# Sixteen of 256 tokens taken out of the dense first expert product in both layers, their gathered dots issued in steps on separate tiles

## Chip, core and metric

One core of a Trainium2 chip runs the whole program. The metric is device time in microseconds (us) of one execution. Three runs of the kernel before took 1743.48, 1745.44 and 1746.33 us, so the median is 1745.44 us. One further execution was taken by the profiler: it took 1742.17 us, and its span from the first to the last instruction is 1740.5 us.

## What is computed

A trunk of two layers for 256 tokens of width 1024. Each layer mixes tokens and then sends each token through a retrieval over 16384 single-neuron experts, cut here to what matters:

```python
def block(t):                                   # PEER, per 128 tokens
    q = (t @ w_pq).reshape(T, 8, 2, 128)
    s = einsum('thpk,hpnk->thpn', q, sub_keys)
    ...                                         # top 16 of 128 keys, twice; top 16 of their pairs
    gate = softmax(best_s)
    u = expert_down[experts]                    # (T, 8, 16, D): 128 chosen experts a token
    act = gelu(einsum('td,thkd->thk', t, u))
    vv = expert_up[experts]
    return einsum('thk,thkd->td', gate * act, vv)
```

## The kernel before

The kernel doesn't gather `expert_down` for most tokens. It multiplies all 16384 rows of it with all tokens, applies the gelu, and multiplies the result with a gate that is zero for experts that weren't chosen.

**The first product** (`experts`, the loop over `i` from 0 to 127, here called tiles). A tile is 128 experts. Its 128x1024 matrix comes by DMA (SP's queue), ACT casts it to a high part `hi` (L245), DVE subtracts to get a low part `lo` (L238), and PE makes 24 products of 128x128 weights with `width` token columns (L317 hi, L318 lo, L319 hi again, for eight slices of D). Casts are kept about two tiles ahead of PE, in three buffers. Two tiles are a pair and share a PSUM bank. After each pair ACT takes the gelu of the bank: L1030 and L1033 for tokens 0 to 191, L1022 for those from 192 on, which L1023 stores to DRAM as `act_rows`. `FT` gives `width` by layer.

**The fill.** While the first tiles run, DVE still works off the retrieval of the experts (top keys, candidates, ranks; `run_fill`), which ends in `to_picks` with the chosen experts and gates. Only then do gates start. In layer 0, DVE also makes 48 conditioning dots (L203) among the tiles from 24 on; in layer 1 only 8.

**Gates.** For tokens 0 to 191, in 48 groups of four, GpSimd (POOL) makes four one-hots of 128x128 (L992), DVE makes three more tiles (L995, L997 twice), PE multiplies them (L1005, L1006, eight products a group) and DVE and ACT use the result (L1013, L1016, L1041). There are two buffers for one-hots, so group g+2's are made after group g's products.

**The remaining 64 tokens** are not gated densely. Their 128 chosen rows of `expert_up` are fetched by POOL with indirect DMAs (`fetch`, L1074), 128 of them in a layer, and their activations are read back out of `act_rows` (`fetch_act`, L1081).

**The dot path.** With `width` 240, the last 16 tokens are left out of the dense product. In layer 1 before, their 16x128 activations come by gathering: 128 partitions hold 16 tokens by 8 heads, and each of 16 steps `k` gathers 128 rows of `down_rows`, 512 KB, with an indirect DMA on POOL (`dot_fetch`, L949) into one of three buffers `R_DOTS`, and multiplies and sums it with the tokens' own rows `R_DX` on DVE (`dot`, L955). Gather k+3 goes to the buffer of dot k, so it waits for it. To get `R_DX`, DVE adds the two halves of the tokens (L933), PE transposes them in eight products (L937), ACT copies them (L938), and ACT's queue writes them to DRAM and reads them back eight times (L939, L943). The ranks take the same way (L940, L944), and DVE makes row numbers of them (L945, the wait of the first gather). Afterwards ACT takes the gelu (L959) and eight more DMAs bring the activations to where the second product uses them (L965). `dot_start` issues all of the preparation at one tile, `dot_step` a dot every two and a half tiles.

**What sets the order.** The program states the work in the order above, but a scheduler moves each instruction to the earliest place that its own model of time allows, by engine, except where `manual_schedule` holds. Each engine then works its queue strictly in that order. So the tile at which the program writes a step bounds it little; the built order tells where it stands.

## Time and profile before

| | |
|---|---|
| profiled execution, its span | 1742.17 us, 1740.5 us |
| median of three runs | 1745.44 us |
| busy: PE, DVE, ACT, POOL | 1702.8, 1454.1, 906.4, 878.6 us |
| first product of layer 0 (width 256), first to last pair's gelu | 196.8 to 583.9 us |
| first product of layer 1 (width 240), first to last pair's gelu | 1047.7 to 1434.4 us |
| one dot on DVE, one gather's issue on POOL, mean | 1257 ns, 1408 ns |
| a gather from issue to landing, median | 6.3 us |

A group's row in the lists reads: line, engine, operation, output<-input, shape, count | busy us, mean ns of one | the engine's idle time just before them and what ended it. A row of the timeline reads: start us, length us, engine, line, operation, count, and in brackets the idle time before it. In the table of windows each stretch has its length, then busy us and the number of instructions of each engine, then PE's granted clock (1.00 is full), the DMA share and GB/s. The two layers' first products are the same work but for width and the dot path, so their stretches can be laid side by side.

### The profile page before, as it was taken

What the parts mean: (1) busy time and instruction counts of PE and PEld (TensorE: products, weight loads), DVE (VectorE), ACT (ScalarE), POOL (GpSimd) and SP (SyncE); (2) the same over time, 40 slices, a digit from 0 to 9 for tenths busy, and PEclk for the clock granted to TensorE, in tenths of its full rate; (3) what the DMA queues carried; (4) which work ended last, traced back from release to release, by engine and by line L of the source; (5) the groups of instructions that cost most, each with busy time, mean ns of one, the idle gap of its engine ahead of it and who ended that gap; (6) DMA issues with size and microseconds to landing.
All of it is one profiled execution on the core that took longest, in us unless ns stands there. A gap on an engine that the chain in (4) does not pass through costs nothing.

```text
span 1740.5 us, 32411 instructions
## 1 busy us (share of the span) xinstructions
PE 1702.8 (98%) x11856; PEld 1556.9 (89%) x11856; DVE 1454.1 (84%) x2722; ACT 906.4 (52%) x1472; POOL 878.6 (50%) x713
## 2 busy tenths in 40 slices
PE   7999999999999999999999999998899999999998
PEld 6889999999999888888888999997899998888887
DVE  6858998788889799999966699957878877999996
ACT  2446455555444555555557555553455455555553
POOL 1000206588998477676100012339989847877630
PEclk9999999999999999999999999998999999999999
DMA  9965578888878799999843556677866667999993
GB/s 381 339 237 173 163 209 280 304 261 255 258 249 262 238 349 402 366 354 384 324 151 121 170 160 181 213 241 239 290 206 194 211 202 252 394 399 350 369 371 114
DMA packets 162563, 461.94 MB, mean 265 GB/s; under 512 B 51586, under 2 KB 53010, under 8 KB 161251
## 3 DMA queue, kind: packets, MB, share of 16 engines
q1 hardware_dynamic: 99936, 363.38, 61.6%
q0 software_dynamic: 26240, 88.36, 13.6%
q10 hardware_dynamic: 36226, 8.13, 2.2%
q8 instruction: 93, 1.52, 0.4%
q14 instruction: 68, 0.55, 0.1%
HBM read 449.16 MB, written 10.57 MB: 264 GB/s over the span
## 4 chain that ended last, share of the span: by engine, by line
PE 85%; DVE 9%; DMA 3%; issue 1%; ACT 1%; POOL 1%; ACTq 0%; SPq 0%; DVEq 0%; POOLq 0%
PE acc L1115 34%; PE ch L317 13%; PE ch L318 13%; PE ch L319 12%; DVE lo L238 3%; PE ch L315 3%; DMA arena<-in_down_rows,arena 1%; PE ch L398 1%; PE g L1005 1%; PE g L1006 1%; DMA raw<-in_w_ada 1%; PE acc L317 1%; PE acc L319 1%; PE acc L318 1%; DVE arena L780 1%
## 5 line engine op out<-in xcount | busy, mean ns | idle before, releaser
L245 ACT CAST hi<-raw 128x1024 fp32r<-128x1024 f32 x554 | 582.1, 1051 | 611.1 <-PE ch L319 318.4
L238 DVE TENSOR_TENSOR lo<-raw,hi 128x1024 fp32r<-128x1024 f32 x554 | 675.8, 1225 | 152.4 <-ACT hi L245 150.5
L318 PE MATMUL ch<-hh,lo 128*128 128x256 f32 (+1 forms) x2336 | 657.2, 281 | 11.9 <-DVE lo L238 11.8
L317 PE MATMUL ch<-hh,hi 128*128 128x256 f32 (+1 forms) x2336 | 661.7, 284 | 1.8 <-ACT ungated L1022 1.8
L319 PE MATMUL ch<-hh,hi 128*128 128x256 f32 (+1 forms) x2336 | 654.2, 280 | 0.0
L992 POOL TENSOR_SCALAR arena<-iota,picks 128x128 f16<-128x128 f16 x384 | 451.7, 1193 | 184.2 <-PE g L1006 82.1
L318 PEld LDWEIGHTS ch<-hh,lo 128*128 128x128 f32 x2336 | 443.7, 190 | 14.5 <-DVE lo L238 14.3
L317 PEld LDWEIGHTS ch<-hh,hi 128*128 128x128 f32 x2336 | 443.2, 190 | 2.3 <-ACT ungated L1022 2.0
L319 PEld LDWEIGHTS ch<-hh,hi 128*128 128x128 f32 x2336 | 443.7, 190 | 0.0
L1115 PE MATMUL acc<-hi,hh 128*128 128x512 f32 x1536 | 400.1, 395 | 0.0
L1115 PEld LDWEIGHTS acc<-hi,hh 128*128 128x128 f32 x1536 | 289.2, 188 | 67.3 <-DVE hh L1056 0.2
L1115 PE MATMUL acc<-lo,hh 128*128 128x512 f32 x1024 | 280.9, 395 | 0.0
L1074 POOL DMA_INDIRECT arena<-in_up,arena x128 | 184.3, 1440 | 107.3 <-DVE arena L1111 79.1
L1115 PEld LDWEIGHTS acc<-lo,hh 128*128 128x128 f32 x1024 | 192.9, 188 | 45.0
L1081 POOL DMA_INDIRECT arena<-act_rows,arena x128 | 178.8, 1397 | 83.2 <-PE acc L1115 45.1
L1111 DVE SCALAR_TENSOR_TENSOR arena<-arena 128x1024 f32<-128x1024 f32 x126 | 162.0, 1286 | 2.0 <-DMA arena<-in_up,arena 2.0
L203 DVE SCALAR_TENSOR_TENSOR raw<-raw,arena 128x1024 f32<-128x1024 f32 x96 | 116.8, 1221 | 9.9 <-DMA raw<-in_w_ada 5.8
L794 POOL CAST arena<-arena 128x512 f16<-128x512 uint32 x32 | 29.2, 926 | 139.2 <-DVE arena L783 107.6
L997 DVE TENSOR_TENSOR arena<-arena,parts 128x512 f16<-128x512 f16 x192 | 77.2, 441 | 21.4 <-PE g L1005 21.4
L758 POOL DMA_DIRECT2D arena<-in_keys x2 | 1.1, 562 | 169.7 <-issue 117.2
L1016 ACT ACTIVATE arena<-g 128x344 f32<-128x344 f32 (+23 forms) x96 | 31.1, 324 | 82.1 <-DVE arena L1013 80.3
L1056 DVE TENSOR_TENSOR hh<-arena,hh 128x768 fp32r<-128x768 f32 (+1 forms) x66 | 61.6, 933 | 0.9 <-ACT hh L1054 0.9
(243 smaller groups left out, 1656.5 us busy)
## 6 DMA issues: line engine op xcount, KB each, us to landing
raw<-in_down SPq DMA_DIRECT2D x256, 512.0 KB, 4.4
raw<-in_up SPq DMA_DIRECT2D x256, 512.0 KB, 6.3
raw<-in_w_ada SPq DMA_DIRECT2D x96, 512.0 KB, 4.9
raw<-in_w_pq SPq DMA_DIRECT2D x32, 512.0 KB, 3.8
raw<-in_w_in SPq DMA_DIRECT2D x26, 512.0 KB, 4.4
raw<-in_w_out SPq DMA_DIRECT2D x16, 512.0 KB, 3.9
act_rows<-ungated ACTq DMA_DIRECT2D x64, 64.0 KB, 4.7
arena<-in_w_in SPq DMA_DIRECT2D x6, 512.0 KB, 9.2
```

What stands on the lines that cost most here:

```text
L203: op = nc.vector.scalar_tensor_tensor(raw, raw, 1.0, cact, op0=OP.mult, op1=OP.mult, accum_out=mods[layer][:, col:col + 1])
L238: nc.vector.tensor_sub(lo, raw, hi.bitcast(F32))
L245: nc.scalar.copy(hi, raw)
L317: nc.tensor.matmul(dst, hi[:, cols], k[0], start=start, stop=False, **kw)
L318: nc.tensor.matmul(dst, lo[:, cols], k[0], start=False, stop=False, **kw)
L319: nc.tensor.matmul(dst, hi[:, cols], k[1], start=False, stop=stop, **kw)
L992: nc.gpsimd.tensor_scalar(oh[:, i, :], iota, picks[:, t:t + 1], None, op0=OP.is_equal)
L997: nc.vector.tensor_tensor(og[j], on, wide(1 + j), op=OP.mult)
L1074: nc.gpsimd.indirect_dma_start(out=R_ROWS[slots[k]], out_offset=None, in_=rows, in_offset=bass.IndirectOffsetOnAxis(ap=where_row[:, k:k + ...
L1081: nc.gpsimd.indirect_dma_start(out=R_ACTS[:, k % (2 * GROUP), :width - T], out_offset=None, in_=act_rows[layer][:, :], in_offset=bass.Indi ...
L1111: nc.vector.scalar_tensor_tensor(R_SUM, v, w8[:, k:k + 1], R_SUM, op0=OP.mult, op1=OP.add)
L1115: nc.tensor.matmul(acc[piece], w, u[:, lo:hi], start=piece not in opened, stop=last, skip_group_check=True)
```

## The change

`FT` becomes 240 in both layers, so layer 0 gets the dot path too. The bundle `dot_start` is cut into steps: `dot_rows` at tile 4, the store of the rows at tile 6, `dot_spread` at tile 9; after the fill (tile `start`) the store of the ranks, `dot_ranks` two tiles later, `dot_where` four later, the first three gathers at five, six and seven. Dot k stands at `start + 9 + 25k/8` and issues gather k+3 itself. Gelu and read-back follow. Three small regions move to another place in the arena, so that they can be written while the fill runs.

```diff
-FT = (S, 240)
+FT = (240, 240)
+DOT_STEP = 25
...
-        def dot_start():
+        def dot_rows():
             nc.vector.tensor_add(R_DH, hh[:, 0, :, width:].bitcast(F32), hh[:, 1, :, width:].bitcast(F32))
             for half in range(2):
...
                 nc.scalar.copy(R_DX[:alone, half * 512:(half + 1) * 512], ps[:alone, :])
-            nc.scalar.dma_start(dot_in, R_DX[:alone, :])
-            nc.scalar.dma_start(dot_ids, chosen[P - alone:, 0, :])
+        def dot_spread():
             for h in range(8):
-                t = slice(h * alone, (h + 1) * alone)
-                nc.scalar.dma_start(R_DX[t, :], dot_in)
-                nc.scalar.dma_start(R_DIX[t, 0, :], dot_ids[:, 16 * h:16 * h + 16])
+                nc.scalar.dma_start(R_DX[h * alone:(h + 1) * alone, :], dot_in)
+        def dot_ranks():
+            for h in range(8):
+                nc.scalar.dma_start(R_DIX[h * alone:(h + 1) * alone, 0, :], dot_ids[:, 16 * h:16 * h + 16])
+        def dot_where():
             nc.vector.tensor_scalar(R_DIX[:, 1, :].bitcast(U32), R_DIX[:, 0, :], float(layer * P * P), None,
                                     op0=OP.add)
+            nc.vector.memset(R_DA, 0.0)
...
                                            accum_out=R_DIX[:, 2, k:k + 1])
+            if k + 3 < 16:
+                dot_fetch(k + 3)
...
-            if n % 5 or n < 0:
-                return
-            k = n // 5
-            if k == 0:
-                dot_start()
-                for m in range(3):
-                    dot_fetch(m)
-            elif 3 <= k < 19:
-                dot(k - 3)
-                if k < 16:
-                    dot_fetch(k)
-            elif k == 19:
-                dot_end()
+        def dot_plan(start):
+            plan = {start: [lambda: nc.scalar.dma_start(dot_ids, chosen[P - alone:, 0, :])],
+                    start + 2: [dot_ranks], start + 4: [dot_where]}
+            for k in range(3):
+                plan[start + 5 + k] = [lambda k=k: dot_fetch(k)]
+            for k in range(16):
+                plan.setdefault(start + 9 + k * DOT_STEP // 8, []).append(lambda k=k: dot(k))
+            end = start + 9 + 15 * DOT_STEP // 8
+            plan[end + 1] = [dot_acts]
+            plan[end + 3] = [dot_back]
+            return plan
+        dots = {}
+        if alone:
+            dots = {4: [dot_rows], 6: [lambda: nc.scalar.dma_start(dot_in, R_DX[:alone, :])], 9: [dot_spread]}
...
-            if alone and start is not None:
-                for n in range(2):
-                    dot_step(2 * (i - start) + n)
+            if alone and start == i + 1:
+                dots.update(dot_plan(i + 1))
+            for fn in dots.pop(i, ()):
+                fn()
```

How the built order moves. POOL's queue in layer 0, kernel before, from the end of the fill: L992 is the one-hots, L1074 the fetches of `expert_up` rows, L1081 the reads of activations in the second product.

```order
L893 DMA x_dram<-arena 128x2048
L794 CAST arena<-arena 128x512 x16
L992 TENSOR_SCALAR arena<-iota,picks 128x128 x12
L1074 DMA arena<-in_up,arena 128x1024 x4
L992 TENSOR_SCALAR arena<-iota,picks 128x128 x180
L1081 DMA arena<-act_rows_102,arena 128x64 x16
```

The same place in the changed kernel, where the one-hots are L1000 and the gathers for dots L953:

```order
L1000 TENSOR_SCALAR arena<-iota,picks 128x128 x12
L953 DMA arena<-in_down_rows,arena 128x1024 x5
L1000 TENSOR_SCALAR arena<-iota,picks 128x128 x4
L953 DMA arena<-in_down_rows,arena 128x1024
L1000 TENSOR_SCALAR arena<-iota,picks 128x128 x3
L953 DMA arena<-in_down_rows,arena 128x1024
L1000 TENSOR_SCALAR arena<-iota,picks 128x128
L953 DMA arena<-in_down_rows,arena 128x1024
L1000 TENSOR_SCALAR arena<-iota,picks 128x128 x8
L953 DMA arena<-in_down_rows,arena 128x1024
L1000 TENSOR_SCALAR arena<-iota,picks 128x128 x4
L953 DMA arena<-in_down_rows,arena 128x1024
```

Sixteen gathers now stand among the one-hots of groups 3 to 13, and the four first fetches of `expert_up` rows, which stood ahead of group 3, stand among those of groups 14 to 17. The one-hots between the first gather and the last of these four fetches are 56, that is 14 groups.

POOL's queue in layer 1, kernel before, from the first one-hots to the twelfth gather:

```order
L992 TENSOR_SCALAR arena<-iota,picks 128x128 x8
L949 DMA arena<-in_down_rows,arena 128x1024 x3
L992 TENSOR_SCALAR arena<-iota,picks 128x128 x12
L949 DMA arena<-in_down_rows,arena 128x1024 x3
L992 TENSOR_SCALAR arena<-iota,picks 128x128 x8
L949 DMA arena<-in_down_rows,arena 128x1024
L992 TENSOR_SCALAR arena<-iota,picks 128x128 x4
L949 DMA arena<-in_down_rows,arena 128x1024 x2
```

The same place in the changed kernel:

```order
L1000 TENSOR_SCALAR arena<-iota,picks 128x128 x12
L953 DMA arena<-in_down_rows,arena 128x1024 x10
L1000 TENSOR_SCALAR arena<-iota,picks 128x128 x4
L953 DMA arena<-in_down_rows,arena 128x1024
L1000 TENSOR_SCALAR arena<-iota,picks 128x128 x4
L953 DMA arena<-in_down_rows,arena 128x1024 x2
L1000 TENSOR_SCALAR arena<-iota,picks 128x128 x8
L953 DMA arena<-in_down_rows,arena 128x1024
```

Ten gathers now stand in one piece ahead of the one-hots of group 3, where three stood ahead of group 2 before.

DVE's queue in layer 1, kernel before, at the first dots (L955; L238 is `lo`):

```order
L1013 SCALAR_TENSOR_TENSOR arena<-arena,g 128x46x4
L955 SCALAR_TENSOR_TENSOR arena<-arena 128x1024 x3
L995 TENSOR_TENSOR arena<-iota_87,parts 128x512
L238 TENSOR_TENSOR lo<-raw,hi 128x1024 x2
L203 SCALAR_TENSOR_TENSOR raw,mod_113<-raw,arena 128x1024
L1041 TENSOR_TENSOR arena<-arena,gt 128x2x12
L955 SCALAR_TENSOR_TENSOR arena<-arena 128x1024
```

And in the changed kernel (L959 is the dot, L239 `lo`, L948 the row numbers):

```order
L948 TENSOR_SCALAR arena<-arena 128x16
L239 TENSOR_TENSOR lo<-raw,hi 128x1024 x2
L959 SCALAR_TENSOR_TENSOR arena<-arena 128x1024
L239 TENSOR_TENSOR lo<-raw,hi 128x1024
L959 SCALAR_TENSOR_TENSOR arena<-arena 128x1024
L239 TENSOR_TENSOR lo<-raw,hi 128x1024
L959 SCALAR_TENSOR_TENSOR arena<-arena 128x1024
L239 TENSOR_TENSOR lo<-raw,hi 128x1024
L959 SCALAR_TENSOR_TENSOR arena<-arena 128x1024
```

The first dot stood behind the uses of the first three gate groups and three dots came together; now it stands right behind the row numbers, ahead of the `lo` of tile 40, and dots and `lo` take turns. By the order the 16 dots of layer 1 stand among the `lo` of tiles 40 to 58, and those of layer 0 among the `lo` of tiles 44 to 65; before, those of layer 1 stood among the `lo` of tiles 49 to 63.

More of the change, by code (lines that the diff above doesn't have):

```diff
@@ L151, in hybrid_trunk @@
     R_DX = region(108 * S, D)
-    R_DIX = region(121 * S, 4, 16)
-    R_DA = region(121 * S + 64, TS)
-    R_DH = region(121 * S + 128, DC, 16)
+    R_DIX = region(127 * S + 128, 4, 16)
+    R_DA = region(127 * S + 192, TS)
+    R_DH = region(127 * S, DC, 16)
     R_S = region(80 * S, 2, 16, P)
@@ L927, in experts @@
         alone = S - width
-        dots = deque()
-        def dot_start():
+        def dot_rows():
             nc.vector.tensor_add(R_DH, hh[:, 0, :, width:].bitcast(F32), hh[:, 1, :, width:].bitcast(F32))
@@ L956, in dot, with dot_acts, dot_back @@
                                            accum_out=R_DIX[:, 2, k:k + 1])
-        def dot_end():
+            if k + 3 < 16:
+                dot_fetch(k + 3)
+        def dot_acts():
             nc.scalar.activation(R_DIX[:, 3, :], R_DIX[:, 2, :], AF.Gelu)
             nc.scalar.dma_start(dot_out, R_DIX[:, 3, :])
-            nc.vector.memset(R_DA, 0.0)
+        def dot_back():
             for half in range(2):
@@ L966, in dot_end @@
                                         dot_out[at:at + alone, :])
-        def dot_step(n):
-            if n % 5 or n < 0:
-                return
-            k = n // 5
-            if k == 0:
-                dot_start()
-                for m in range(3):
-                    dot_fetch(m)
-            elif 3 <= k < 19:
-                dot(k - 3)
-                if k < 16:
-                    dot_fetch(k)
-            elif k == 19:
-                dot_end()
+        def dot_plan(start):
[8 more added lines that the diff above has]
+            plan[end + 3] = [dot_back]
+            assert end + 3 < 108
+            return plan
+        dots = {}
+        if alone:
+            dots = {4: [dot_rows], 6: [lambda: nc.scalar.dma_start(dot_in, R_DX[:alone, :])], 9: [dot_spread]}
         def make_onehots(g):
```

## The prediction

> **What bounds the kernel now.** I read the page first, then the groups by shape, then stretches of the two first products, then the queues where a stretch is slow. The page says that PE is all but full:
>
> ```profile
> PE 1702.8 (98%) x11856; PEld 1556.9 (89%) x11856; DVE 1454.1 (84%) x2722; ACT 906.4 (52%) x1472; POOL 878.6 (50%) x713
> PE 85%; DVE 9%; DMA 3%; issue 1%; ACT 1%; POOL 1%; ACTq 0%; SPq 0%; DVEq 0%; POOLq 0%
> ```
>
> So columns taken from PE shorten the kernel, if nothing else falls behind. The gelu of the last tokens (L1022) comes once a pair of tiles; its count in windows that begin and end on one gives the pace. The first two windows are layer 0, with 256 columns, before gates and with them; the last three are layer 1, with 240:
>
> ```profile
> 196.70:312.40 115.70, 5.39 (x20) 1.00 0.77 243
> 312.40:583.80 271.40, 11.99 (x43) 1.00 0.82 258
> 1047.60:1157.70 110.10, 4.83 (x20) 1.00 0.69 213
> 1157.70:1245.20 87.50, 2.79 (x11) 0.94 0.76 245
> 1245.20:1434.30 189.10, 8.03 (x32) 1.00 0.69 213
> ```
>
> Layer 0 takes 115.70 / 20 = 5.79 us a pair, then 271.40 / 43 = 6.31 with gates. Layer 1 takes 5.51 and 5.91 (189.10 / 32), so narrow tiles are worth 0.28 and 0.40 us a pair. But its middle window takes 87.50 for 11 pairs, where 11 x 5.91 = 65.0 would do: 22.5 us are lost there, and there the dots are. The groups by shape name who is late:
>
> ```profile
> L318 PE MATMUL ch<-hh,lo 128*128 128x256 f32 x1312 | 372.5, 284 | 0.1
> L318 PE MATMUL ch<-hh,lo 128*128 128x240 f32 x1024 | 284.7, 278 | 11.8 <-DVE lo L238 11.8
> L955 DVE SCALAR_TENSOR_TENSOR arena<-arena 128x1024 f32<-128x1024 f32 x16 | 20.0, 1257 | 13.1 <-DMA arena<-in_down_rows,arena 12.5 <-DMA arena<-dot_in 0.5
> L949 POOL DMA_INDIRECT arena<-in_down_rows,arena x16 | 22.5, 1408 | 17.7 <-issue 16.7 <-DVE lo L238 0.3 <-DVE arena L1013 0.3
> ```
>
> PE waits 11.8 us for `lo` at 240 columns, 0.1 at 256. DVE sits 12.5 us at dots whose gathers haven't landed, and `lo` is queued behind them. The gathers are late because of POOL's queue, here without the rows between:
>
> ```profile
> 1145.14 1.27 POOL L949 DMA_INDIRECT arena<-in_down_rows,arena  x1 [14.21 <-issue]
> ...
> 1172.29 5.59 POOL L992 TENSOR_SCALAR arena<-iota,picks 128x128 f16<-128x128 f16 x4 [2.23 <-PE g L1006]
> 1178.03 1.57 POOL L949 DMA_INDIRECT arena<-in_down_rows,arena  x1 [0.16 <-issue]
> ...
> 1183.31 7.86 POOL L992 TENSOR_SCALAR arena<-iota,picks 128x128 f16<-128x128 f16 x8
> 1191.34 1.01 POOL L949 DMA_INDIRECT arena<-in_down_rows,arena  x1 [0.17 <-issue]
> 1192.38 5.69 POOL L992 TENSOR_SCALAR arena<-iota,picks 128x128 f16<-128x128 f16 x4
> ...
> 1247.98 37.86 POOL L992 TENSOR_SCALAR arena<-iota,picks 128x128 f16<-128x128 f16 x36
> ```
>
> The first gathers go at 1145, but the fourth at 1178: it needs dot 0, which waited for its tokens' rows, and it stands behind three groups of one-hots. From then to 1248 one-hots and indirect DMAs follow each other without a pause. Late PE then also runs slower; its clock is the third column from the end:
>
> ```profile
> 1180.00:1200.00 20.00, 16.02 (x127) 15.19 (x128) 16.85 (x32) 6.69 (x13) 19.30 (x16) 0.91 0.80 268
> 1200.00:1220.00 20.00, 16.19 (x129) 15.73 (x128) 11.43 (x21) 6.22 (x12) 18.76 (x21) 0.83 0.75 247
> ```
>
> 0.91 and 0.83 are 20 x (0.09 + 0.17) = 5.2 of the 22.5 us. The waits of layer 1 (total, times, longest) are short ones:
>
> ```profile
> PE ch L318 <- DVE lo L238: 11.8, 9, 2.5
> ```
>
> **The change part by part.**
>
> *Layer 0's width.* 20 pairs x 0.28 = 5.6, 44 pairs (the last lies past the window) x 0.40 = 17.6: 23.2 us off PE, on the path. The eight transposes are new in layer 0, twice this row, 1.2 us on PE:
>
> ```profile
> 1160.82 0.60 PE L937 MATMUL g<-ident,arena 128*16 128x128 f32 x4
> L943 ACTq DMA_DIRECT2D arena<-dot_in x8: 327/432/1477, 1167.3 to 1172.1; - x8
> ```
>
> The 27 DMAs that ACT's queue issues for the dot path are at 0.43 us each 11.6 us of ACT, which has half its time free (52% busy) and keeps two tiles ahead: nothing, unless all stand before one cast, which they don't: the order puts at most five in a row.
>
> *Layer 0's fill.* The fill already fills DVE in layer 1, at the pace that I use. Layer 0 has conditioning dots beside it, from tile 24 on. These rows count L203 in the two layers, each with a read of 0.08 us, so 48 and 8:
>
> ```profile
> 191.00:587.00 396.00, 58.87 (x96) 1.00 0.79 252
> 1042.00:1438.00 396.00, 10.15 (x16) 0.99 0.70 219
> ```
>
> Seven of them (58.87 / 48 = 1.23 us each) fall before the fill's end, 8.6 us of DVE. Most of it delays only the fill; the bounds are 0 and 8.6, and I take 2, nearer to 0, since `lo` stands ahead of the fill's later steps in the queue.
>
> *Layer 0's dots, on POOL.* In the order, the changed kernel has on POOL, from the first gather to the last of the first four up-fetches, 20 indirect DMAs and 56 one-hots, and then group 17's four. Prices, from stretches with one-hots (first layer 0, then layer 1 at the dots, then layer 1 after them), and of the gathers:
>
> ```profile
> 319.90:565.00 245.10, 213.38 (x180) 1.00 0.82 256
> 1159.60:1243.10 83.50, 54.79 (x48) 0.94 0.75 242
> 1247.90:1416.10 168.20, 146.75 (x136) 1.00 0.69 213
> 1178.00:1230.00 52.00, 18.38 (x13) 0.90 0.73 244
> ```
>
> A group is 213.38 / 45 = 4.74, 54.79 / 12 = 4.57 and 146.75 / 34 = 4.32 us; an indirect DMA 18.38 / 13 = 1.41. So 20 x 1.41 + 15 x 4.74 = 99.3 us, and some 4 us at the start, where the fourth gather waits for dot 0 and so for a landing:
>
> ```profile
> DMA to landing us min/median/max: 4.4/6.3/10.1
> ```
>
> PE wants group 17 before tile 70, by its order. POOL begins when PE is at about tile 40: in layer 1 the first gather went 12.6 us before tile 42 (1145.14 to 1157.70), at tile 37.4, and the ranks' DMAs stand three casts later in layer 0. From there 4 tiles at 2.75 and 26 at 2.96 are 88 us. POOL is 103 - 88 = 15 us late, and PE's gate products stand in its queue ahead of the next tile. Before, POOL had none of this in layer 0: its up-fetches went in idle time. Group 17 is the worst place; after it POOL needs 4.74 for each 5.91 us pair and catches up.
>
> *The same dots on DVE.* This row of layer 0 with gates shows DVE busy 213.80 of 244.80 us:
>
> ```profile
> 319.90:564.70 244.80, 244.80 (x2214) 243.12 (x2211) 213.80 (x373) 118.62 (x237) 213.38 (x180) 1.00 0.82 256
> ```
>
> It idles 31 us in 244.80, so 9 in the 71 us of the 24 tiles at the dots (24 x 2.96), of which the faster pace takes 24 x 0.20 = 5. Sixteen dots ask 16 x 1.26 = 20: 16 us too much, about as much as on POOL. The two queues are late beside each other, so I take 17 once, 16 and 1 for the clock. Bounds: one-hots at 4.32 and gathers at the 1.01 of 1191.34 give 20 + 65 + 4 - 88 = 1; the 12.5 us of waits at dots coming on top give 30.
>
> [...] Here the longest wait was 2.5 us and the clock still fell to 0.83. [...]
>
> *Layer 1's dots.* Their tokens' rows are now made in the fill, so dot 0 waits only for its gather: issued at 1145.1 it lands 6.3 later, the dot is done at 1152.7, and the `lo` of tile 40 behind it (1.2 us) at 1153.9, where PE wants it at 1157.7 - 5.5 = 1152.2. That is 1.7 us, with `lo` from this row:
>
> ```profile
> L238 DVE TENSOR_TENSOR lo<-raw,hi 128x1024 fp32r<-128x1024 f32 x554 | 675.8, 1225 | 152.4 <-ACT hi L245 150.5 <-PE acc L1115 0.3
> ```
>
> Then each dot needs the gather that was issued three dots before: 1.4 + 6.3 + 1.26 is 9 us for three, PE takes 3 x 2.75 = 8.3, so DVE keeps up with hardly a reserve. POOL is held at its tenth gather until dot 6, which the order has ahead of the `lo` of tile 46, about when PE is at tile 45.3. From there to group 11's one-hots the order has 10 indirect DMAs and 9 groups: 14.1 + 9 x 4.57 = 55.2 us, and PE wants group 11 before tile 61: 15.7 x 2.96 = 46.5. Late by 9, with the 1.7 about 10, in place of 22.5: a gain of 12.5. Bounds 2 (at 4.32 and 1.01: 49 - 46.5) and 18.
>
> *Small things at nothing:* the read-back of activations is 48 instead of 64 columns, the dots' results return (L965) some 40 tiles before the second product, and the moved regions cost nothing.
>
> Sum: -23.2 + 1.2 + 2 + 17 = -3 in layer 0, -12.5 in layer 1, -15.5 in all. The profiled execution took 1742.2 us, so 1726.7 of its kind; the median lies 3.3 above it, 1745.4 - 15.5 = 1730.
>
> **The rivals.**
>
> *It spreads as written.* Layer 1 loses 2 and layer 0 2 in place of 10 and 17: -15.5 - 8 - 15 = -38.5, 1707 us. For it: the tokens' rows come early, gathers are issued with nothing between. Against: POOL's work above is there wherever it stands. Chance 0.16.
>
> *The steps don't spread.* The scheduler puts the dots where its model sees room, 16 in 19 tiles in layer 1, where before there were 16 in 15; so layer 1 keeps its 22.5 and layer 0 takes its 17: -3, 1742 us. For it: the order. Against: tokens' rows no longer come in between. Chance 0.17.
>
> *Slower: dots hold up the one-hots themselves.* A one-hot lasts from 590 to 2920 ns:
>
> ```profile
> L992 POOL TENSOR_SCALAR arena<-iota,picks x384: 590/870/2920, 271.1 to 1414.6; 128x128 f16<-128x128 f16 x192
> ```
>
> If each dot stops POOL for its length, the lateness grows by 16 x 1.26 = 20 us in layer 0 and, with half of the dots ahead of the groups, by 10 in layer 1: -15.5 + 30 = +14.5, 1760 us. It decides from 0.65 us a dot, where 24 dots use up the 15.5. For it: a group costs 4.74 in the layer with 48 more DVE passes, 4.32 without. Against: at the old dots it is 4.57, so 12 x 0.25 = 3 us for 13 dots, 0.23 each. Chance 0.12. [...]
>
> **How the numbers follow.** The forecast has 0.55. It alone spans 1714 (layer 0 and 1 at 6 and 5 lost) to 1744 (26 and 15). The range reaches into the first rival and to the end where nothing is gained: 1708 to 1746. About 0.2% (3.5 us) can be told from no change. Faster: 0.52 of the forecast, 0.16, 0.07 of the second rival, 0.02 of the last: 0.77. Same: 0.02 and 0.07: 0.09. Slower: 0.14.
>
> **What would show it.** Layer 0's pairs without gates at about 5.5 us (the first step), those after tile 70 at 5.9; between tiles 44 and 70 a window some 17 us too long, with POOL at 95% or more and gates or `lo` waited for. In layer 1 the first dot near 1152 less layer 0's gain, and 10 us lost in place of 22.5. It is wrong if layer 0 shows no slow window (prices of POOL's queue too high), or layer 1 still loses over 18.

## The result, and the profile after

The changed kernel takes 1757.6 us (median of 4 runs, 1755.5 to 1762.3), the kernel before 1745.9 beside it: ratio 1.007, 95% interval 1.005 to 1.009. It is slower, where 1730 was forecast and the range ended at 1746. The profiled execution took 1762.3 us, the longest of the four, with a span of 1760.6, so its stretches may be a few us long. Its page:

```profile
PE 1698.9 (96%) x11864; PEld 1542.8 (88%) x11864; DVE 1474.3 (84%) x2765; ACT 902.8 (51%) x1475; POOL 925.3 (53%) x729
PE 73%; DVE 11%; issue 5%; POOL 4%; DMA 4%; ACT 1%; ACTq 0%; SPq 0%; POOLq 0%; DVEq 0%
```

PE was 85% of the chain that ended last and is 73% now. PE's busy time hardly fell (1702.8 to 1698.9 us) although 16 of 256 columns are gone in layer 0: part of it ran at a lower clock. The stretches between gelus of the last tokens show where (L1030; lines are those of the changed kernel, where a one-hot is L1000, `lo` L239, a conditioning pass L204, a dot L959, a gather L953, a gate product L1013). Columns: window, its length, then busy us (and instructions) of PE, PEld, DVE, ACT, POOL, then PE's clock. The first three windows are layer 0's 20 pairs before gates, the 14 pairs with the dots, the 29 after them; the last three are layer 1's first 18 pairs, the 12 with the dots, the 33 after them:

```profile
198.20:310.70 112.50, 110.54 (x985) 109.54 (x984) 107.50 (x331) 60.31 (x96) 28.55 (x22) 1.00 0.76 236
310.70:419.50 108.80, 91.32 (x799) 87.63 (x798) 91.74 (x162) 42.49 (x88) 99.69 (x82) 0.95 0.87 294
419.50:600.80 181.30, 177.26 (x1638) 174.53 (x1638) 160.79 (x268) 88.00 (x180) 156.88 (x118) 0.98 0.82 263
1066.80:1168.40 101.60, 98.27 (x874) 97.10 (x872) 90.75 (x306) 54.71 (x86) 22.28 (x21) 1.00 0.66 197
1168.40:1260.10 91.70, 81.45 (x703) 78.70 (x704) 68.45 (x118) 36.75 (x75) 74.93 (x65) 0.93 0.84 277
1260.10:1453.50 193.40, 193.40 (x1844) 192.17 (x1843) 152.18 (x251) 99.64 (x203) 144.55 (x136) 1.00 0.68 206
```

Layer 0's dots take 108.80 us for 14 pairs, 26 more than 14 x 5.91 = 82.7. After them, 29 pairs take 181.30, 6.25 each, which is 9 more than 29 x 5.95 = 172.5, a pace that other runs below reach there. Before gates the narrow tiles pay as forecast (112.5 against 115.7). So layer 0's first product takes 402.6 us in place of 387.1. Layer 1's takes 386.7 in place of 386.7, though its steps stand on separate tiles now. What PE waited for in layer 0 (total, times, longest):

```profile
PE g L1013 <- POOL arena L1000: 15.5, 20, 2.1
PE ch L319 <- DVE lo L239: 5.6, 5, 3.2
```

Before, the profile shows no wait of PE in these pairs of layer 0. The one-hots on POOL are the larger part, and the clock (0.95 and 0.98) adds 108.8 x 0.05 + 181.3 x 0.02 = 9 us. The one-hots have become longer: 192 of them take 251.12 us in layer 0, and 209.26 in layer 1 (columns here: POOL's busy time in the one-hots alone):

```profile
265.00:612.00 347.00, 251.12 (x192) 0.98 0.84 274
1010.00:1480.00 470.00, 209.26 (x192) 0.99 0.69 214
```

The kernel before has 234.44 and 217.27 there.

### The profile page after: what moved, and what is told of

Its sections match the earlier page's. It is cut to its first block, busy times and chain, and to the rows that moved or that the text cites. A ratio compares the mean times of both kernels' runs of the same rounds, so it can differ in the third digit from the quotient of the medians.

```text
span 1760.6 us, 32530 instructions
## 1 busy us (share of the span) xinstructions
PE 1698.9 (96%) x11864; PEld 1542.8 (88%) x11864; DVE 1474.3 (84%) x2765; ACT 902.8 (51%) x1475; POOL 925.3 (53%) x729
## 4 chain that ended last, share of the span: by engine, by line
PE 73%; DVE 11%; issue 5%; POOL 4%; DMA 4%; ACT 1%; ACTq 0%; SPq 0%; POOLq 0%; DVEq 0%
PE acc L1123 32%; PE ch L318 10%; PE ch L319 10%; PE ch L320 10%; DVE lo L239 4%; POOL arena L1000 3%; PE ch L316 3%; DMA arena<-in_down_rows,arena 2%; DMA raw<-in_w_ada 1%; PE ch L399 1%; PE g L1013 1%; PE g L1014 1%; POOL arena L1089 1%; DVE arena L784 1%; DVE arena L782 1%
## 5 line engine op out<-in xcount | busy, mean ns | idle before, releaser
L239 DVE TENSOR_TENSOR lo<-raw,hi 128x1024 fp32r<-128x1024 f32 x554 | 676.6, 1227 | 123.5 <-ACT hi L246 122.5
L319 PE MATMUL ch<-hh,lo 128*128 128x240 f32 (+1 forms) x2336 | 654.1, 280 | 11.3 <-DVE lo L239 11.0
L318 PE MATMUL ch<-hh,hi 128*128 128x240 f32 (+1 forms) x2336 | 655.7, 282 | 1.4 <-ACT hi L246 1.0
L320 PE MATMUL ch<-hh,hi 128*128 128x240 f32 (+1 forms) x2336 | 649.8, 278 | 0.0
L1000 POOL TENSOR_SCALAR arena<-iota,picks 128x128 f16<-128x128 f16 x384 | 460.4, 1214 | 142.4 <-DVE picks L866 108.4
L1089 POOL DMA_INDIRECT arena<-act_rows,arena x128 | 191.9, 1500 | 87.0 <-PE acc L1123 48.9
L1082 POOL DMA_INDIRECT arena<-in_up,arena x128 | 187.2, 1462 | 87.9 <-DVE arena L1119 62.9
L204 DVE SCALAR_TENSOR_TENSOR raw<-raw,arena 128x1024 f32<-128x1024 f32 x96 | 117.7, 1231 | 9.9 <-DMA raw<-in_w_ada 6.1
L795 POOL CAST arena<-arena 128x512 f16<-128x512 uint32 x32 | 25.3, 803 | 136.7 <-DVE arena L784 105.5
L1005 DVE TENSOR_TENSOR arena<-arena,parts 128x512 f16<-128x512 f16 x192 | 79.2, 451 | 19.1 <-PE g L1013 19.0
L1013 PE MATMUL g<-arena 128*128 128x128 f16 x384 | 58.5, 224 | 24.4 <-POOL arena L1000 23.2
```

What stands on the lines that cost most here:

```text
L204: op = nc.vector.scalar_tensor_tensor(raw, raw, 1.0, cact, op0=OP.mult, op1=OP.mult, accum_out=mods[layer][:, col:col + 1])
L239: nc.vector.tensor_sub(lo, raw, hi.bitcast(F32))
L318: nc.tensor.matmul(dst, hi[:, cols], k[0], start=start, stop=False, **kw)
L319: nc.tensor.matmul(dst, lo[:, cols], k[0], start=False, stop=False, **kw)
L320: nc.tensor.matmul(dst, hi[:, cols], k[1], start=False, stop=stop, **kw)
L1000: nc.gpsimd.tensor_scalar(oh[:, i, :], iota, picks[:, t:t + 1], None, op0=OP.is_equal)
```

## The experiments

First one table. Times are medians (us), each ratio is to runs of the kernel before that were taken beside the kernel's own. The stretches are those above, from one profiled execution of each kernel: all of the layer's first product, layer 0's 14 pairs at the dots and 29 after them, layer 1's 12 pairs at the dots. In the paced kernels (e12, e10, e14) the dots reach into the 29 pairs. "One-hots" is POOL's busy time in layer 0's one-hots, 192 unless noted, where the little by which they overlap counts once (the expectations add up single instructions, 253.8 in place of 251.1).

| kernel | time | ratio to before, 95% | layer 0 | 14 pairs | 29 pairs | one-hots | layer 1 | 12 pairs |
|---|---|---|---|---|---|---|---|---|
| before | 1745.9 | | 387.1 | 88.2 | 183.2 | 234.4 | 386.7 | 90.5 |
| after | 1757.6 | 1.005–1.009 | 402.6 | 108.8 | 181.3 | 251.1 | 386.7 | 91.7 |
| e1 layer 1 only | 1740.3 | 0.996–0.999 | 386.6 | 88.2 | 183.1 | 234.5 | 382.9 | 86.6 |
| e2 layer 0 only | 1759.2 | 1.005–1.010 | 402.1 | 109.8 | 180.0 | 253.7 | 386.8 | 74.7 |
| e3 no gathers | 1739.1 | 0.994–0.997 | 394.3 | 101.4 | 180.6 | 254.2 | 375.6 | 78.5 |
| e4 short dots | 1746.4 | 0.999–1.002 | 398.4 | 108.6 | 177.4 | 235.1 | 376.1 | 79.2 |
| e7 neither | 1723.0 | 0.984–0.989 | 381.2 | 89.6 | 179.2 | 247.2 | 372.5 | 75.4 |
| e8 dots, one input | 1739.7 | 0.995–0.998 | 391.3 | 99.4 | 179.6 | 240.9 | 381.1 | 84.1 |
| e9 conditioning, one input | 1742.0 | 0.996–1.000 | 387.6 | 102.8 | 172.5 | 197.9 | 384.9 | 88.9 |
| e13 both, one input | 1728.4 | 0.988–0.992 | 380.4 | 95.2 | 172.6 | 187.2 | 377.4 | 82.4 |
| e5 half on VectorE | 1735.4 | 0.993–0.996 | 384.8 | 100.2 | 171.9 | 121.6 (x96) | 379.0 | 81.8 |
| e6 dots' groups on VectorE | 1742.2 | 0.996–1.000 | 393.9 | 101.6 | 179.9 | 182.6 (x132) | 377.2 | 80.2 |
| e11 before, half on VectorE | 1740.8 | 0.996–0.999 | 388.1 | 88.2 | 183.2 | 123.5 (x96) | 381.9 | 84.3 |
| e12 paced | 1750.2 | 1.000–1.004 | 401.2 | 92.7 | 195.0 | 244.4 | 377.1 | 70.6 |
| e10 paced, half on VectorE | 1722.9 | 0.984–0.990 | 383.2 | 89.0 | 181.0 | 151.3 (x96) | 369.7 | 70.3 |
| e14 paced, a quarter in layer 0 | 1721.7 | 0.984–0.988 | 380.3 | 87.0 | 180.9 | 197.4 (x144) | 372.5 | 70.3 |

(Layer 1 of e2 has 256 columns and no dots.)

### One layer alone

e1 gives layer 0 all its columns back:

```diff
-FT = (240, 240)
+FT = (S, 240)
```

> Width 256 in layer 0 again, the new steps in layer 1 alone. Theory P (POOL's queue: one-hots come late because indirect DMAs share the queue with them, layer by layer): layer 0's first product is back at 387 us and layer 1's stays at 387, so 1746 us, within 3. Theory D (DVE: dots and waits ahead of the low parts, which also leave later work behind): the same layer 0, and 1746 too. A coupling between the layers (layer 1 slow only because layer 0 was) would give under 1735.

e2 does the reverse; the two DRAM tiles of the dot path are sized by layer 0:

```diff
-FT = (240, 240)
+FT = (240, S)
```

> The new steps in layer 0 alone, width 256 without dots in layer 1. Layer 1 took as long with 240 columns and dots as layer 0 with 256 and none, so both theories P and D expect about the time of the changed kernel, 1758 us, within 4: the narrow columns of layer 1 are worth nothing. If layer 1's dots do pay, it is over 1770.

The new steps in layer 1 alone gain about 4 us, layer 0 alone loses 14. So the loss is layer 0's. e1's time is some 3 us under the band of both theories, but over that of a coupling. What layer 1 gains in e1 (386.7 to 382.9) it doesn't gain in the changed kernel. And layer 1 without any dots and with 256 columns takes 386.8 us, as much as before with 240 columns: the dots cost there what the columns brought.

### Gathers away, dots shortened, both

e3 issues no gathers:

```diff
-            nc.gpsimd.indirect_dma_start(
-                out=R_DOTS[k % 3], out_offset=None, in_=down_rows[:, :],
-                in_offset=bass.IndirectOffsetOnAxis(ap=R_DIX[:, 1, k:k + 1].bitcast(U32), axis=0))
+            pass
...
-            nc.vector.scalar_tensor_tensor(row, row, 1.0, R_DX, op0=OP.mult, op1=OP.mult,
+            nc.vector.scalar_tensor_tensor(row, R_DX, R_DIX[:, 1, k:k + 1], R_DX, op0=OP.mult, op1=OP.mult,
```

> The 32 gathers for dots are left out, and each dot multiplies the tokens' rows with themselves and a row number, so that its DVE pass has the same size and still follows the row numbers; the 16 tokens' activations are not the right ones. P: POOL has only its one-hots and fetches, layer 0 loses 5 and not 38 us, layer 1 5 and not 22: 1758 - 50 = 1708 us, up to 1720 since the dots now stand closer together on DVE. D or L (dots lengthen the one-hots): the dots are all there, so at most the waits for gathers go (29.7 us of DVE): over 1738 us.

e4 keeps the gathers and multiplies 8 of 1024 columns:

```diff
-            nc.vector.scalar_tensor_tensor(row, row, 1.0, R_DX, op0=OP.mult, op1=OP.mult,
+            nc.vector.scalar_tensor_tensor(row[:, :8], row[:, :8], 1.0, R_DX[:, :8], op0=OP.mult, op1=OP.mult,
```

> The dots multiply 8 columns and not 1024, the gathers are as they were; the 16 tokens' activations are not the right ones. P: POOL's queue has the same 40 indirect DMAs among the same one-hots, so little changes: 1747 to 1758 us. D: 32 x 1.15 = 37 us of DVE go, most of them from the two slow stretches: under 1730 us. L: one-hots in the slow stretch of layer 0 fall from 1.16 to under 1.0 us each, and the time to about 1735.

e7 does both.

> The changed kernel without the 16 gathers of each layer and with dots over 8 columns instead of 1024 (both left out at once, so the gathered tokens' activations are wrong; their transposes, small DMAs and the reading back of results stay). Layer 0's first product takes 402.6 us in the changed kernel, layer 1's 386.7; at the paces of the prediction, without any loss, 63 pairs are 20 x 5.51 + 43 x 5.91 = 364. Theory PD (the issue of gathers on POOL and the passes of the dots on DVE are together the whole loss): both layers at 362 to 370, so 1757.6 - 35 - 20 = about 1700, between 1694 and 1708. Theory F (layer 0's narrow tiles don't reach layer 1's pace there, because its 48 conditioning dots stay on DVE beside a faster PE): layer 1 at 362 to 370, layer 0 at 378 or more, so 1712 to 1722, with waits for lo and for one-hots spread over layer 0.

Without gathers 18 us come back, with short dots 11, with both 35, five more than the sum. e3's time is just over the bound of theories D and L, e4's just under theory P's band: each theory had said that one of the two would do most, and both queues count. In e3 the one-hots are as long as with gathers, in e4 they are 16 us shorter.

In layer 0's 14 pairs alone the parts don't add up: e3 gives back 7.4 us, e4 nothing (108.6), e7 19.2. So there the loss to one queue mostly remains when only the other's work is taken away. The comparison isn't clean, for the scheduler builds another order when gathers or long dots are gone: in e4 gathers often stand two together, and at its dots PE waits for ACT (6.1 us), `lo` (5.4) and one-hots (3.9), with DVE far from full (columns as in the stretches above):

```profile
309.40:418.00 108.60, 93.00 (x811) 89.63 (x810) 76.36 (x168) 43.95 (x88) 90.70 (x86) 0.94 0.87 310
```

e7 shows what only its own theory F supposed: layer 0 without any gather or long dot still takes 381.2 us, and its 29 later pairs 179.2. (Its time is 1 us over F's band.) PE waits in layer 0 for one-hots, 8.0 us in 15 times:

```profile
PE g L1011 <- POOL arena L998: 8.0, 15, 1.3
```

Narrow tiles in layer 0 alone are therefore worth 387.1 - 381.2 = 6 us, not 23. Something other than the dots makes one-hots long in layer 0.

### What a pass reads

The trace shows it in single instructions. This is DVE in a stretch of the changed kernel some 30 us after the dots (columns: start, length in us), and the one-hot that ran on POOL beside it:

```profile
446.85 1.21 DVE L239 TENSOR_TENSOR lo<-raw,hi 128x1024 fp32r<-128x1024 f32 x1
447.98 1.22 DVE L204 SCALAR_TENSOR_TENSOR raw<-raw,arena 128x1024 f32<-128x1024 f32 x1
449.12 0.08 DVE L204 DVE_READ_ACCUMULATOR raw<-raw,arena 128x1 f32 x1
...
446.90 2.67 POOL L1000 TENSOR_SCALAR arena<-iota,picks 128x128 f16<-128x128 f16 x1
```

A one-hot of 0.59 us (the shortest) lasts 2.67: it starts 0.05 us after the `lo`, sits through that and through the conditioning pass right behind it, and ends at 449.57, 0.4 us after the second. Over all 192 one-hots of layer 0, a least-squares fit of length to overlap with DVE's work gives some 0.45 us, plus 0.8 us for each us of `lo` beside it, 0.8 of a conditioning pass, 0.65 of a dot, 0.4 to 0.7 of the gates' smaller passes that read two tensors of SBUF (L1003, L1005), but only 0.1 to 0.3 of the multiplication with the gates (L1021), which reads one tensor of SBUF and one of PSUM. It explains 96% of the variance; its second digits depend on how the small passes are grouped. A long one-hot overlaps more work anyway, so a fit alone proves little. e8 and e9 test it: the pass stays as long but reads one tensor of SBUF.

e8, the dots:

```diff
-            nc.vector.scalar_tensor_tensor(row, row, 1.0, R_DX, op0=OP.mult, op1=OP.mult,
-                                           accum_out=R_DIX[:, 2, k:k + 1])
+            nc.vector.tensor_scalar(row, row, 1.0, None, op0=OP.mult, op1=OP.add,
+                                    accum_out=R_DIX[:, 2, k:k + 1])
```

> The changed kernel with each dot's pass over 1024 columns as a scaling of the gathered row with its sum, which reads one tensor of SBUF instead of two (the product with the token is left out, so the gathered tokens' activations are wrong); gathers, waits and order stay nearly as they are. Theory L (a dot that reads two tensors holds up POOL's one-hots): layer 0's one-hots, 253.8 us in all in the changed kernel, come down to 240 or less, as with dots over 8 columns (238.6), and the time to 1745 to 1750. Theory D (the dots cost by their time on DVE, ahead of the low parts of tiles): the pass is about as long (1.0 to 1.3 us), so the one-hots stay at 250 or more and the time at 1754 to 1761.

e9, the conditioning passes:

```diff
-        op = nc.vector.scalar_tensor_tensor(raw, raw, 1.0, cact, op0=OP.mult, op1=OP.mult,
-                                            accum_out=mods[layer][:, col:col + 1])
+        op = nc.vector.tensor_scalar(raw, raw, 1.0, None, op0=OP.mult, op1=OP.add,
+                                     accum_out=mods[layer][:, col:col + 1])
```

> The changed kernel with all 96 conditioning passes on DVE (48 of them beside layer 0's first product) as a scaling of the weight row with its sum, which reads one tensor of SBUF instead of two (the product with the condition is left out, so every modulation is wrong). The dots, gathers and one-hots are those of the changed kernel. Theory L (while a DVE pass reads two tensors of SBUF, a one-hot on POOL stands still): layer 0's one-hots come from 253.8 us down by some 0.8 x 45 us of overlap to 210 to 225, its pairs after the dots from 6.25 to about 5.95 us, and the time to 1736 to 1746. Theory D (a pass costs by its time on DVE): the pass lasts as long (1.2 us), so one-hots stay at 248 or more and the time at 1753 to 1762.

The passes keep their length, 1208 ns for 1226 in the dots:

```profile
L959 DVE TENSOR_SCALAR_CACHE_REDUCE arena<-arena x32: 1205/1208/1223, 314.9 to 1217.8; 128x1024 f32<-128x1024 f32 x32
```

```profile
L959 DVE SCALAR_TENSOR_TENSOR arena<-arena x32: 1209/1226/1544, 315.7 to 1239.3; 128x1024 f32<-128x1024 f32 x32
```

Yet 18 us go in e8 and 15.6 in e9. e9 is the cleaner of the two: up to the end of the dots, layer 0's order on POOL and DVE is that of the changed kernel. In e8 (and in e13 below) a fetch of `expert_up` rows moved ahead of the gathers, and later gathers stand elsewhere among the one-hots. The same place in e9, first DVE, then two one-hots:

```profile
440.63 1.21 DVE L239 TENSOR_TENSOR lo<-raw,hi 128x1024 fp32r<-128x1024 f32 x1
441.77 1.21 DVE L204 TENSOR_SCALAR_CACHE_REDUCE raw<-raw 128x1024 f32<-128x1024 f32 x1
...
440.77 1.54 POOL L1000 TENSOR_SCALAR arena<-iota,picks 128x128 f16<-128x128 f16 x1
...
442.30 0.60 POOL L1000 TENSOR_SCALAR arena<-iota,picks 128x128 f16<-128x128 f16 x1
```

The first one-hot still lasts 1.54 us beside the `lo`, but ends at 442.31, beside the pass, and the next takes 0.60 us beside it. In all, 26 one-hots of e9 lie wholly within a conditioning pass, and they take 0.59 to 0.60 us. Layer 0's one-hots fall from 251.12 to 197.89 us, and the 29 pairs after the dots run without a wait, 172.5 us at full clock (POOL's one-hots alone, then the stretch with all engines):

```profile
265.00:612.00 347.00, 197.89 (x192) 0.99 0.85 284
```

```profile
413.30:585.80 172.50, 172.50 (x1638) 171.35 (x1638) 158.30 (x268) 88.17 (x181) 115.02 (x116) 1.00 0.83 275
```

DVE is busy 158.30 us there, against 160.79 in the changed kernel, so DVE's time isn't what changed; POOL's is, 115.02 for 156.88. That is theory L, with the one-hots lower than it said (198, or 201 as the expectations count, for 210 to 225). In e8 theory L missed its bands, by 5 us in the time (faster) and by 4 in the one-hots (243.9 as the expectations count, for 240 or less), but theory D is further off. The fit's price for the replaced pass falls to about 0.3 in both.

e13 has both edits.

> The changed kernel with both kinds of passes, the 96 conditioning passes and the 32 dots, as scalings with a sum that read one tensor of SBUF (both products are left out, so modulations and gathered tokens' activations are wrong); gathers and one-hots as in the changed kernel. Alone the two gave 15.6 us (conditioning, nearly all of it in layer 0) and 17.9 us (dots, 11 in layer 0, 6 in layer 1). Theory L (passes that read two tensors stop the one-hots, and that is the loss): layer 0's one-hots at 185 to 197 us, layer 0 at 368 to 378, layer 1 at 378 to 383, 1722 to 1730. Theory Q (beside that, gathers and one-hots share POOL's queue at the dots, which stays the bound whatever the passes read): layer 0 stays at 383 to 388 as with the conditioning alone, 1734 to 1741.

Its layer 0, the 14 pairs at the dots and the 29 after them, and what PE waited for in it:

```profile
309.40:404.60 95.20, 86.28 (x799) 83.25 (x797) 91.43 (x164) 43.69 (x87) 76.97 (x83) 1.00 0.96 342
404.60:577.20 172.60, 172.60 (x1641) 171.47 (x1639) 158.36 (x269) 88.00 (x180) 117.43 (x116) 1.00 0.85 273
```

```profile
PE ch L319 <- DVE lo L239: 10.1, 12, 1.8
```

The time, 1728.4, lies where theory L had it; layer 0 (380.4) lies between the bands of the two theories. Of layer 0's loss of 26 + 9 = 35 us, what the passes read accounts for some 402.6 - 380.4 = 22 (15 of them in e9, with the order unchanged). The other 12.5 us (95.2 - 82.7) stand at the dots. There PE waits for `lo` and no longer for one-hots, DVE is busy 91.43 of 95.20 us, and the clock is whole, which points to DVE's own time.

### Taking the one-hots off POOL

e5 makes two one-hots of each group of four on VectorE:

```diff
-                nc.gpsimd.tensor_scalar(oh[:, i, :], iota, picks[:, t:t + 1], None, op0=OP.is_equal)
+                eng = nc.vector if i < 2 else nc.gpsimd
+                eng.tensor_scalar(oh[:, i, :], iota, picks[:, t:t + 1], None, op0=OP.is_equal)
```

> The changed kernel with the first two one-hots of every group of four made on VectorE, the others on POOL as before. POOL then has half of its 4.66 us a group. Theory P (POOL's queue is the bound at the dots): layer 0's slow pairs 20 to 34 lose under 10 in place of 26 us, layer 1 under 12 in place of 22, so 1725 to 1738. Theory D (DVE is as full as POOL there): two one-hots at 0.2 to 0.3 us for each of 47 groups add some 20 us to DVE in each layer, the waits move from the one-hots to lo, and the time stays at 1752 or goes over 1760.

e6 makes all those of groups 3 to 17 there (the condition is `3 <= g < 18` in place of `i < 2`).

> The changed kernel with all the one-hots of groups 3 to 17 made on VectorE, those after them on POOL as before: at the dots POOL then issues gathers and up-fetches and nothing else. Theory P: the loss at the dots goes (layer 0 26 to under 8, layer 1 22 to under 8) and gathers no longer wait in the queue: 1720 to 1732. Theory D: 60 one-hots at 0.2 to 0.3 us are 12 to 18 us more on DVE within the very stretch where it has the dots: PE then waits for lo or one-hots on DVE, 1750 to 1765.

e11 is e5's edit on the kernel before.

> The kernel before, with the first two one-hots of each group on VectorE and nothing else. If the 22 us that half of the one-hots gave the changed kernel come from a lock that the change tightened, this one gains little: layer 0, which waits for nothing before, stays at 386 to 388, layer 1 gets some of its 22 us back: 1735 to 1743, and the change made on top of it is worth about nothing to 8 us. If moving one-hots is worth the same everywhere, 1720 to 1728.

On DVE a one-hot takes 0.26 us (e5, median; the longest 0.39):

```profile
L1001 DVE TENSOR_SCALAR arena<-iota,picks x192: 239/256/386, 272.5 to 1399.8; 128x128 f16<-128x128 f16 x192
```

e5 is 22 us faster than the changed kernel and 0.55% faster than the kernel before, and its 29 later pairs run at 171.9. At the dots it still loses 17 us, more than theory P allowed: PE waits there for `lo` (10.1 us) and no longer for one-hots. e6 falls between its theories: where it puts 60 one-hots on a DVE that has the dots, PE waits for `lo` (10.5 us), and later groups still wait for POOL (5.4). e11 gains 4 us, all in layer 1: without narrow tiles layer 0 has no wait to lose. So the change is worth about 1740.8 - 1735.4 = 5 us once POOL is relieved; the two ratios to the kernel before have intervals that just overlap.

### Spreading the dots for good

The order has the 16 dots in some 20 tiles although the plan has 47 (that was the second rival's argument). e12 ties each dot to its tile: ScalarE writes the dot's factor of 1.0 after a gelu near the planned tile.

```diff
-            nc.vector.scalar_tensor_tensor(row, row, 1.0, R_DX, op0=OP.mult, op1=OP.mult,
+            nc.vector.scalar_tensor_tensor(row, row, R_DIX[:, 3, k:k + 1], R_DX, op0=OP.mult, op1=OP.mult,
...
+                ones[at // 2 - 1] = k
...
+            if pair in ones:
+                k = ones[pair]
+                nc.scalar.activation(R_DIX[:, 3, k:k + 1], ps[:, 0:1], AF.Copy, scale=0.0, bias=1.0)
```

> The changed kernel with each dot's factor of 1.0 written by ScalarE right after the gelu of the pair before the dot's planned tile, so that the dots spread over some 47 tiles; all one-hots on POOL. Theory L (POOL's one-hots, stretched by DVE's passes, are the bound in layer 0): POOL has 254 us of one-hots and some 22 of gathers there against 264 us of PE, so layer 0 still loses 15 or more and stays at 386 or more, while layer 1 (212 + 22) comes to 368 to 374: 1726 to 1740. Theory B (bunching is all): both layers at 366 to 372, 1708 to 1718. Theory N (the work costs the same wherever it stands): 1750 to 1760.

e10 is e12 with e5's edit.

> Half of the one-hots on VectorE (as in the run with that alone, 1735.4 us), and each dot's factor of 1.0 is now written by ScalarE right after the gelu of the pair before the dot's planned tile, so that dots and gathers can't go earlier than planned and spread over some 47 tiles. Theory B (what is left of the loss there, 13 us in layer 0 and 7 in layer 1, is the bunching of the dots in 20 tiles): 1712 to 1722. Theory N (what is left is the sum of DVE's and POOL's work in the product, wherever it stands): 1730 to 1738.

e14 is e10 with one one-hot of four on VectorE in layer 0 (`i < 1 + layer`).

> The paced dots with half of the one-hots on VectorE (1722.9 us), where layer 0 has only the first one-hot of each group of four on VectorE, layer 1 still two. In that run DVE was busy 151.31 of 151.80 us at layer 0's dots, and POOL 94.14. Theory D (layer 0 is now bound by DVE): 48 one-hots at 0.26 us are 12 us less on DVE, POOL has the room, and layer 0 comes from 383 to 370 to 377: 1711 to 1718. Theory L2 (a third one-hot on POOL, at 1.3 to 1.6 us under the lock, brings POOL's queue back as the bound): PE waits for one-hots again and the time stays at 1720 or more.

Spreading alone moves the loss and doesn't end it: in e12 layer 0's 14 pairs come down to 92.7 us and the next 29 go up to 195.0. PE waits for one-hots for 14.7 us in those 29, and for 19.8 in all of layer 0:

```profile
PE g L1016 <- POOL arena L1003: 19.8, 20, 2.4
```

Layer 1, which has few conditioning passes, gains 10 (3 fewer than theory L's band). The time lies in theory N's band and above theory L's, yet the layers split much as L had it. With POOL relieved as well, e10 reaches 1722.9 us, 1 us over theory B's band and 1.3% faster than before, and PE no longer waits for one-hots. Layer 0's rest is DVE, busy 151.31 of 151.80 us at the spread dots:

```profile
418.20:570.00 151.80, 145.04 (x1356) 141.64 (x1355) 151.31 (x299) 71.29 (x156) 94.14 (x61) 1.00 0.87 288
```

e14 takes 48 one-hots off DVE and gets only 3 us of layer 0 for it (380.3), while layer 1 takes 3 us longer (372.5): 1721.7 us. Its runs (1721.3 to 1723.1) overlap e10's (1721.9 to 1725.5), so the two can't be told apart. DVE is still busy 149.52 of the 151.80 us:

```profile
418.20:570.00 151.80, 146.33 (x1371) 143.42 (x1370) 149.52 (x268) 70.98 (x155) 117.80 (x85) 1.00 0.87 290
```

Theory D missed. Theory L2 has the time and the renewed waits for one-hots, but they are only 3.4 us, and DVE stays nearly full beside them.

## Why the prediction was wrong

The two profiled executions differ by +20 us, where -15.5 was forecast. Of these 36 us, 18.5 stand in layer 0 (15.5 lost, 3 forecast as gain), 12.5 in layer 1 (nothing gained), and 5 outside the two first products, where nothing was expected. The medians differ by less, 11.7.

**Right: layer 0's width and fill.** The 20 pairs before gates took 112.5 us: at layer 1's pace 110.1, so the fill cost 2.4 where 2 was taken.

**Right: POOL's prices at the dots.** In layer 0's dot stretch a group took 4.66 us and an indirect DMA 1.39, where 4.74 and 1.41 were taken. From the first gather (307.2) to group 17's last one-hot (416.9) POOL needed 110 us: 100 of work, as the sum had it (99.3), and 9 of pauses, where 4 was taken. PE had room for 88.

**Failed in size: "so I take 17 once, 16 and 1 for the clock".** The stretch lost 26. PE stood idle in it for 17.5 us (11.4 for one-hots, 3.8 for `lo`, 1.0 each for `hi` and a gate tile), close to the 16. But the 1 us for the clock was an estimate that no run shows: the clock took 108.8 x 0.05 = 5.4, and 3 us more aren't accounted for. Whether the queues' terms may be taken once isn't settled. The 14 pairs lose 18.7 us without gathers (e3), 25.9 with short dots (e4), 12.5 with one-input passes (e13), 6.9 with neither gathers nor long dots (e7): taking away the work of one queue leaves most of the loss, but the built orders of these kernels differ.

**Failed: "after it POOL needs 4.74 for each 5.91 us pair and catches up".** This is the step where the prediction lacked a cause: one-hots that last longer beside VectorE's passes that read two tensors (2.67 us for 0.59 above, some 0.8 us for each us of `lo` or conditioning pass by the fit). First, PE's order wants more than a group a pair: in the changed kernel the first products of groups 18 and 47 stand 51 tiles apart, which is 29 groups in 25.5 pairs, so pairs of 5.91 us leave POOL 5.2 us a group. Second, a group took 5.3 us there (156.88 / 29.5), so POOL never caught up, and another 9 us went, 3.6 of them by the clock. The 4.74 was a price at a pace that left POOL pauses. Here are the same 29 pairs of the kernel before, and of e7, which has narrow tiles but neither gathers nor long dots:

```profile
400.70:583.90 183.20, 183.20 (x1644) 181.73 (x1643) 158.94 (x268) 88.22 (x180) 147.09 (x120) 1.00 0.81 253
399.90:579.10 179.20, 174.12 (x1643) 170.84 (x1642) 160.20 (x268) 87.15 (x179) 156.73 (x120) 1.00 0.79 256
```

Before, a group took 147.09 / 30 = 4.90 us, and POOL waited 17.2 us for PE in between; it waited 3.2 in e7 and 1.6 in the changed kernel. DVE's busy time is nearly the same. But passes that ran in POOL's pauses cost nothing, and now they meet one-hots: the overlap of this stretch's one-hots with `lo` and conditioning passes is 80 us before and 92 in the changed kernel, and 0.8 us for each of these 12, as the fit has it, is an estimate of 10 us, by which the one-hots did grow. So a faster PE made POOL slower, and e7 shows it without the dots. e9 and e13 leave the conditioning passes only one input and get all 9 us back.

**Failed: layer 1 "loses 10".** Its 30th pair came 193.3 us after the first, where 110.1 + 10 x 5.91 = 169.2 is the pace: 24 lost, as against 20.5 before, and over the 18 that the prediction named as a sign of being wrong. The start was later and slower than "1.7 us". POOL's queue in layer 1:

```profile
1167.47 1.77 POOL L953 DMA_INDIRECT arena<-in_down_rows,arena  x1 [11.22 <-DVE arena L948]
...
1194.85 1.68 POOL L953 DMA_INDIRECT arena<-in_down_rows,arena  x1 [1.90 <-DVE arena L959]
1196.57 6.61 POOL L1000 TENSOR_SCALAR arena<-iota,picks 128x128 f16<-128x128 f16 x4
```

The first gather goes 100.7 us into the product, 3.3 later than assumed. Ten gathers hold POOL for 29 us until the first one-hots, where about 22 was assumed, because each waits for a dot, each dot for a landing (6.8 us, not 6.3), and the `lo` behind the dots is late (5.5 us of PE's waits; 7.8 go to one-hots). "DVE keeps up with hardly a reserve" was too tight by 7 us, about one landing. e3 and e4 get 11 of the 24 back each and e7 14, so the late path runs through gathers and dots alike. The passes' two inputs are a smaller part here: e13 gets 9 back; e10, with spread dots and half of the one-hots on VectorE, 17.

**The rivals.** The third had the time (1760) and the family of the cause, with a chance of 0.12. That it hit the time is in part luck, for it laid 30 us on the dots alone. e8 puts the dots' part at 11 + 6 us (with the order changed); the 15 us of conditioning passes, which the change doesn't touch, weren't in any case of mine. It had been argued down with averages, 4.57 at the old dots against 4.32 after them, "0.23 each". That comparison was unfair: at the old dots PE was late, so less of `lo` fell on each one-hot (0.34 us of overlap, 0.43 after them), and a part of what the dots added was hidden by what was missing. The shortest and longest one-hot, 590 and 2920 ns, had been quoted and only the means were used.

Single instructions show of other passes what the rival supposed of dots: a one-hot of 0.59 us lasted 2.67 beside a `lo` and a conditioning pass, which read two tensors of SBUF, and 0.59 to 0.60 within e9's passes, which read one. The other way little is lost: of the 0.60 us of a one-hot that started first, `lo` lost at most some 0.15 us (last section). I had supposed a stop for the dots only and not for the `lo`, which has two inputs as well.

The second rival is half true: steps are bunched, and e12 shows that unbunching alone gains 7 us. The first is out: nothing spread as written, and e12's spread dots still lost in layer 0.

**What stays open.** The 12.5 us at layer 0's dots in e13 are put down to DVE by its busy share and PE's waits; e4 shortened DVE's work there, but in another order and with new waits, and gained nothing in these pairs. Why the clock fell is open too: in layer 0's last 29 pairs it fell twice for 3.4 us to half, where PE's longest pause was 0.7 us and all of them made 4.0. Why e1 gains 4 us in layer 1 that the changed kernel doesn't show wasn't tested.

## What to carry to other kernels

Before you price an engine's work by its mean from a trace, look at the spread of single instructions and lay the long ones beside what the other engines run at that moment. A price that contains what other engines' passes add can rise with the pace, so speeding up the bound engine can make a neighbour the bound: here a group of one-hots went from 4.90 to 5.3 us. To see whether a queue can catch up, count what the bound engine asks of it per step in the built order, and don't take one for one. Where two late queues feed one engine, taking away the work of one may give back little: here, of 26 us, 7.4 in e3 and none in e4, but 19.2 in e7.

## What the runs showed of the hardware

A one-hot on POOL (128x128, f16) took 0.59 to 0.62 us where no VectorE instruction ran beside it (38 of them in the changed kernel), 2.67 across two VectorE passes that read two SBUF tensors, and 0.59 to 0.60 within a pass of the same length with one SBUF input (26 of them in e9). The same one-hot took 0.26 us on VectorE (median of 192 in e5).

VectorE lost little. In layer 0's stretch with gates of the changed kernel, the 70 `lo` passes that began while a one-hot was running took 1.215 us (median; the longest 1.33), the 11 with no one-hot beside them 1.224 (median). In layer 1 of the changed kernel, from 1299 to 1412 us, only a `lo` that came right behind the start of an undisturbed one-hot took over 1.25 us: 1.35 to 1.36 at 0.08 to 0.09 us behind it, 1.26 to 1.29 at 0.15 to 0.18, and 1.21 to 1.23 from 0.29 on.

TensorE's clock fell repeatedly in layer 0: to a mean of 0.95 over the 108.8 us at the dots, where the longest wait was 3.2 us, and of 0.98 over the 181.3 us after them, where PE's longest pause was 0.7. In e12 it had a mean of 0.96 over the 195 us after its 34th pair, and the longest wait for a one-hot was 2.4 us.
